# A hybrid block's input projection: column tiles in pairs by one level of Strassen's product

## The chip, the core and the metric

The kernel runs on one core of a Trainium2 chip. Five engines work side by side and wait for each other by semaphores: TensorE (PE, matmuls), VectorE (DVE), ScalarE (ACT), GpSimd (POOL), and SyncE (SP), which issues the transfers between memory (HBM) and the on-chip buffer (SBUF). PE writes its results into eight banks of PSUM. The metric is device microseconds (us) of the core.

## The reference

x has 1024 tokens of 1024 channels, in float32. What is computed:

```python
h = rmsnorm(x, norm_gain)                       # per token, over 1024 channels
q, f_logit, i_in, z_a, u, gate_b, gate_c, z_b = split(h @ w_in)   # 8 parts of 512 columns
f = lb + (1 - lb) * sigmoid(f_logit);  k = 1 - f
# group A, 4 heads of 128: S_t = diag(f_t) S_{t-1} + k_t v_t^T (v = i_in),  o_t = S_t^T q_t
o_a = grouped_rmsnorm(o_a, hgrn_norm_gain, 4) * silu(z_a)
# group B: causal convolution over 3 tokens, channel by channel
y_b = gate_b * conv3(gate_c * u)
o_b = grouped_rmsnorm(y_b, conv_norm_gain, 8) * silu(z_b)
x = x + concat(o_a, o_b) @ w_out
out = rmsnorm(x, final_norm_gain)
```

The input projection is 1024 x 1024 by 1024 x 4096: 32 column tiles of 128.

## The kernel before

Every product is made from rounded parts: an operand is split into a high part (a cast on ACT) and a low part (source minus high part, on DVE), and a product takes three matmuls: high by high, high by low, low by high. "Main matmul" is one of these, 512 columns wide.

*Stage v* (lines 116 to 173) computes i_in (called v) with tokens on the partitions, the contraction outermost, in all eight PSUM banks: 192 main matmuls, while x and the first weights arrive. x carries the norm's gain but is not normalised: the sums of squares of its rows come from eight further loads of x (`row_sum`, L152), and rst, the inverse root mean square of each token, is applied to the results, as a scale on ACT where tokens are on the partitions, or as a product with R (rst along the columns, L219) where channels are.

*Heads* (`head`, L239): for each of four heads the tiles f and q by `project` (L226: 24 main matmuls for one column tile and one half of the tokens, into one of four banks `psa`), then the recurrence's chain on DVE (sigmoid, a scan L257, four reciprocals L260) and POOL. The recurrence itself is eight small steps on PE.

*Convolution* (`conv`, L338): tiles u, c, b, z of four channel tiles. The norm of y (L362) sums squares over channels by two matmuls with a block of ones (`bones`), for which the squares are split as well (POOL, L377 and L381), then a root on ACT, a reciprocal of 128 x 512 on DVE (L368) and a product.

*Gate z_a and output projection* (L446 to L517): z_a with tokens on the partitions, transposes, then 16 output tiles of 24 main matmuls, residual and final norm; the last tile in two halves.

PE and SP work in the order of the program (`manual_schedule`); a scheduler sets the order on ACT, DVE and POOL. Each engine takes its instructions in its fixed order, so one that waits holds back what stands behind it. `Stream` (L37) sets PE's order: `pe.mm` is a main matmul, `pe.later(n, fn)` puts small steps behind n more of them (STEP 13 between steps of a recurrence, NLAG 44 from a conv tile to its norm's sums). Weights come by `fetch` in 512 KB units, six of them on chip.

Of the kernel before, what the change touches and what calls it, by code (L numbers as in the profile page):

```python
# [16 lines left out]
P = 128  # L17
# [4 lines left out]
W = 512  # L22
# [3 lines left out]
WB = 6       # weight units on chip  # L26
# [29 lines left out]

@with_exitstack
def hybrid_block(ctx: ExitStack, tc: tile.TileContext, xT, x, wtok, wcol, wout, cols, hgain, fgain, out):
# [25 lines left out]
    ga = const.tile([P, W], F32, name="ga")  # L84

# [1 line left out]
    units = [("v", kp, wtok[0, kp]) for kp in range(4)]  # L87
    for h in range(NH):
        units += [("f", h, wcol[2 * h + 1]), ("q", h, wcol[2 * h])]
    for j in range(4):  # L90
        units += [(c, j, wcol[8 + 4 * j + i]) for i, c in enumerate("ucbz")]
    units += [("za", kp, wtok[1, kp]) for kp in range(4)]
    units += [(f"o{n}", kp, wout[n, kp]) for n in range(2) for kp in (2, 3, 0, 1)]
    split, issued = {}, [0]

    def split_part(hi, lo, raw):
        A.copy(hi, raw)
        V.tensor_tensor(lo, raw, hi.bitcast(F32), op=ALU.subtract)  # L98

    def fetch(upto):  # L100
        while issued[0] < min(upto, len(units)):
            c, i, src = units[issued[0]]
            raw = stage.tile([P, 2 * W], F32, tag="st", name=f"raw_{c}{i}")
            hi = wpool.tile([P, 2 * W], F32R, tag="wh", name=f"wh_{c}{i}")
            lo = wpool.tile([P, 2 * W], F32R, tag="wl", name=f"wl_{c}{i}")
            nc.sync.dma_start(raw, src)
            split_part(hi, lo, raw)
            split[c, i] = hi, lo
            issued[0] += 1

    def need(c, i):
        pos = next(p_ for p_, u in enumerate(units) if u[0] == c and u[1] == i)
        fetch(pos + WB)
        return split[c, i]

# [1 line left out]
    pv = [(psa if t < 4 else psb).tile([P, W], F32, tag="ps", name=f"pv{t}") for t in range(NT)]  # L117

    def split_x(k, raw, t0, t1):
        g = col[:, C_NG + k:C_NG + k + 1]  # L120
        rv = raw.rearrange("p (t c) -> p t c", c=P)[:, t0:t1]
        A.activation(XH[:, t0:t1, k, :], rv, AF.Copy, scale=g)
        V.scalar_tensor_tensor(XL[:, t0:t1, k, :], rv, g, XH[:, t0:t1, k, :].bitcast(F32), op0=ALU.mult,
                               op1=ALU.subtract)

    rstart = const.tile([P, W], F32, name="rstart")
    V.memset(rstart[:, :P], 0.0)
    V.memset(rstart[:, P:], 0.0)
    for _ in range(NWARM):  # warms TensorE up while the first loads run
        T.matmul(pv[NT - 1][:, :P], rstart[:, :P], rstart[:, :P], start=True, stop=True)  # L130

    raw = stage.tile([P, S], F32, tag="st", name="rawx0")
    w0 = stage.tile([P, 2 * W], F32, tag="st", name="raw_v0")
    hi = wpool.tile([P, 2 * W], F32R, tag="wh", name="wh_v0")
    lo = wpool.tile([P, 2 * W], F32R, tag="wl", name="wl_v0")
    split["v", 0] = hi, lo
# [12 lines left out]
    ssx = const.tile([P, NT], F32, name="ssx")

    def row_sum(t):
        xr = stage.tile([P, D], F32, tag="st", name=f"xr{t}")  # L152
        nc.sync.dma_start(xr, x[t * P:(t + 1) * P, :])
        A.activation(xr, xr, AF.Square, accum_out=ssx[:, t:t + 1])

    for k in range(NK):
        if k:
            raw = stage.tile([P, S], F32, tag="st", name=f"rawx{k}")
            nc.sync.dma_start(raw, xT[k])
            if k % 2 == 0:  # L160
                fetch(k // 2 + 1)
            split_x(k, raw, 0, NT)
            row_sum(k - 1)
            if k == NK - 1:
                row_sum(k)
                fetch(5)
        hi, lo = split["v", k // 2]
        wh = hi[:, (k % 2) * W:(k % 2 + 1) * W]
        wl = lo[:, (k % 2) * W:(k % 2 + 1) * W]
        for t in range(NT):  # L170
            pe.mm(pv[t], XH[:, t, k, :], wh, start=(k == 0), stop=False)
            pe.mm(pv[t], XH[:, t, k, :], wl, start=False, stop=False)
            pe.mm(pv[t], XL[:, t, k, :], wh, start=False, stop=(k == NK - 1))

# [1 line left out]
    ident = const.tile([P, P], F32, name="ident")  # L176
    make_identity(nc, ident)
# [61 lines left out]
    def head(h):  # L239
# [58 lines left out]
        def combine(pr):  # L298
# [269 lines left out]
```

## Time and profile before

| | us |
|---|---|
| device time, median of 3 runs | 504.24 (502.28 to 506.0) |
| span of the profiled execution | 500.7 |
| own device time of the profiled execution | not among the times shown; the median is 3.54 above its span |
| PE busy | 491.8 (98%) |
| DVE busy | 257.6 (51%) |
| ACT busy | 172.7 (34%) |
| POOL busy | 157.4 (31%) |

The span runs from the first to the last instruction of one execution. Busy time is the time in which an engine executes; register and semaphore instructions don't count. An engine with a low share can still hold back another where its work is due at a certain moment.

### The profile page before, as it was taken

The page shows a single profiled execution, that of the slowest core. Times are in us where ns is not written, and L with a number is a line of the kernel's source. Part 1 is how long each engine was busy: PE and PEld are TensorE (multiplying, and loading weights), DVE is VectorE, ACT ScalarE, POOL GpSimd, SP SyncE. Part 2 cuts the span into 40 slices and gives each one's busy share as a digit, 9 for nine tenths or more (in the row PEclk, how much of TensorE's full clock was granted, in tenths as well). Part 3 has the DMA queues.
Part 4 walks back from the last instruction along what each step waited for, and adds up shares of the span by engine and source line. Part 5 has one row for each costly group of instructions (what it writes and reads, how often), then busy time and mean ns, then how long its engine had stood idle before and what let it go on. Part 6 is the DMA issues. An engine that isn't in the chain of part 4 may idle for free. (4 is left out here: it accounts for less than half of the span.)

```text
span 500.7 us, 5886 instructions
## 1 busy us (share of the span) xinstructions
PE 491.8 (98%) x2288; PEld 402.9 (80%) x2288; DVE 257.6 (51%) x363; ACT 172.7 (34%) x301; POOL 157.4 (31%) x143
## 2 busy tenths in 40 slices
PE   9999999999999999999999999999999999999995
PEld 7778887888888888888888888888888888888884
DVE  4342688948668335285647266552933461132323
ACT  5557722233223223170243127122722341123322
POOL 1000044524315003353658975233432122211000
PEclk9999999999999999999999999999999999999998
DMA  7778621110011110202111111112030171001342
GB/s 218 245 255 258 220 87 43 42 43 13 31 43 43 43 43 8 65 13 85 43 43 42 43 42 42 47 47 76 8 119 0 42 232 42 2 0 63 126 159 93
DMA packets 12699, 38.93 MB, mean 78 GB/s; under 512 B 1536, under 2 KB 2048, under 8 KB 12672
## 3 DMA queue, kind: packets, MB, share of 16 engines
q1 hardware_dynamic: 12672, 38.56, 23.2%
q8 instruction: 18, 0.29, 0.3%
q14 instruction: 9, 0.07, 0.0%
HBM read 34.36 MB, written 4.19 MB: 77 GB/s over the span
## 5 line engine op out<-in xcount | busy, mean ns | idle before, releaser
L44 PE MATMUL po<-wh_o,XL 128*128 128x512 f32 (+1 forms) x136 | 52.0, 382 | 0.0
L44 PE MATMUL po<-wl_o,XH 128*128 128x512 f32 (+1 forms) x136 | 52.0, 382 | 0.0
L44 PE MATMUL po<-wh_o,XH 128*128 128x512 f32 (+1 forms) x136 | 51.9, 382 | 0.0
L253 POOL TENSOR_SCALAR k<-f 128x512 f32<-128x512 f32 x8 | 5.0, 621 | 88.2 <-DVE f L251 88.2
L44 PEld LDWEIGHTS po<-wl_o,XH 128*128 128x128 f32 x136 | 25.5, 188 | 5.5
L44 PEld LDWEIGHTS po<-wh_o,XH 128*128 128x128 f32 x136 | 25.5, 188 | 5.4
L44 PEld LDWEIGHTS po<-wh_o,XL 128*128 128x128 f32 x136 | 25.5, 188 | 5.4
L368 DVE RECIPROCAL rs<-rs 128x512 f32<-128x512 f32 x8 | 26.8, 3353 | 3.7 <-ACT rs L367 3.5
L260 DVE RECIPROCAL ei<-e 128x128 f32<-128x128 f32 x32 | 27.1, 909 | 0.3
L44 PE MATMUL pp_f<-XH,wl_f 128*128 128x512 f32 x64 | 26.3, 411 | 0.0
L44 PE MATMUL pv<-wl_v,XH 128*128 128x512 f32 x64 | 25.6, 400 | 0.6 <-DVE wl_v L98 0.5
L44 PE MATMUL pp_q<-XH,wh_q 128*128 128x512 f32 x64 | 26.0, 407 | 0.0
L44 PE MATMUL pp_f<-XL,wh_f 128*128 128x512 f32 x64 | 26.0, 406 | 0.0
L44 PE MATMUL pp_q<-XH,wl_q 128*128 128x512 f32 x64 | 25.8, 403 | 0.0
L44 PE MATMUL pp_q<-XL,wh_q 128*128 128x512 f32 x64 | 25.8, 403 | 0.0
L44 PE MATMUL pp_f<-XH,wh_f 128*128 128x512 f32 x64 | 25.8, 403 | 0.0
L44 PE MATMUL pza<-wl_za,XH 128*128 128x512 f32 x64 | 25.7, 402 | 0.0
L354 POOL TENSOR_TENSOR cu<-us,R 128x512 f32<-128x512 f32 x8 | 11.3, 1418 | 45.9 <-DVE us L353 45.7
L44 PE MATMUL pv<-wh_v,XH 128*128 128x512 f32 x64 | 25.7, 401 | 0.0
L44 PE MATMUL pp_u<-XH,wl_u 128*128 128x512 f32 x64 | 25.6, 400 | 0.0
L44 PE MATMUL pp_c<-XH,wh_c 128*128 128x512 f32 x64 | 25.5, 399 | 0.0
L44 PE MATMUL pp_u<-XL,wh_u 128*128 128x512 f32 x64 | 25.5, 399 | 0.0
(181 smaller groups left out, 1261.1 us busy)
## 6 DMA issues: line engine op xcount, KB each, us to landing
xr<-x SPq DMA_DIRECT2D x8, 512.0 KB, 4.4
raw_o<-wout SPq DMA_DIRECT2D x8, 512.0 KB, 3.2
xo<-x SPq DMA_DIRECT2D x16, 256.0 KB, 3.4
rawx<-xT SPq DMA_DIRECT2D x7, 512.0 KB, 4.1
out<-y SPq DMA_DIRECT2D x7, 512.0 KB, 2.8
raw_f<-wcol SPq DMA_DIRECT2D x4, 512.0 KB, 3.7
raw_q<-wcol SPq DMA_DIRECT2D x4, 512.0 KB, 5.1
raw_u<-wcol SPq DMA_DIRECT2D x4, 512.0 KB, 3.2
```

What stands on the lines that cost most here:

```text
L44: self.T.matmul(*args, **kw)
L253: G.tensor_scalar(kk, f, -1.0, 1.0, op0=ALU.mult, op1=ALU.add)
L260: V.reciprocal(ei[:, c0:c0 + W // 4], e[:, c0:c0 + W // 4])
L354: G.tensor_tensor(cu[:, 2 + o0:2 + o0 + W], us[hf], rs, op=ALU.mult)
L368: V.reciprocal(rs2, rs2)
```

## The change

x is normalised on the chip before the projections, and 28 of the 32 column tiles (all but v's four) are computed in 14 pairs by Strassen's product in Winograd's form: x transposed is cut into four blocks A11, A12, A21, A22 (two halves of channels by two halves of tokens), a pair's weights into B11, B12, B21, B22 (two halves of channels by two column tiles).

- *x* comes in 16 tiles of 256 KB. In stage v it is used as before, without rst, but one half of the tokens after the other (4 banks each). Its squares (ACT) are added up on POOL; `stats` turns them into rst with four one-column matmuls for each half; `normalise` multiplies x in place by the gain and rst. The eight row loads, R, and its products are gone.
- *Blocks of x*: `split_a` and `x_sums` build seven blocks A11, A12, A22, S1 = A21 + A22, S2 = S1 − A11, S3 = A11 − A21, S4 = A12 − S2, each of four tiles, split into high and low parts (sums on DVE and POOL, casts on ACT, subtractions on DVE or POOL).
- *Weights of a pair* (`prep`): four loads of 256 KB, four sums on POOL (T1 = B12 − B11, T2 = B22 − T1, T3 = B22 − B12, T4 = B21 − T2), seven casts on ACT and seven subtractions on DVE. There are five buffers for high parts, five for low parts, four for raw tiles.
- *A pair* (`pair`): seven products of 12 main matmuls in three banks pb, pa, pd. Three sums are kept: m1 (A11·B11), u2 (pb after S2·T2), m5 (S1·T1) are copied by ACT to SBUF. Each of the four results is a bank plus such a copy, an addition on DVE (L328), or the bank alone. Bank pb takes S2·T2 after m1's copy, S3·T3 after u2's copy, and A22·T4 after the addition in `c22`.
- *Pairs in order*: for each head h the pairs (f, q), (u, c), (b, z) of head h and channel tile h; then z_a in two pairs. So a head and a channel tile now alternate, where all heads came first.
- *Small steps*: STEP 18, NLAG 32 for the first half of a tile and 44 for the second. The norm of a head runs on POOL in the pairs behind it. The output projection loads its weights in 256 KB tiles, and its first job (not the seventh) has two tiles.

```diff
-STEP = 13    # main matmuls between the steps of a head's recurrence
-NLAG = 44    # main matmuls between a conv tile and its norm's sums
...
+STEP = 18
+NLAG = 32, 44
...
-    stage = ctx.enter_context(tc.tile_pool(name="stage", bufs=3))
-    wpool = ctx.enter_context(tc.tile_pool(name="wpool", bufs=WB))
-    tmp = ctx.enter_context(tc.tile_pool(name="tmp", bufs=9))
+    hip = ctx.enter_context(tc.tile_pool(name="hip", bufs=5))
+    lop = ctx.enter_context(tc.tile_pool(name="lop", bufs=5))
+    rawp = ctx.enter_context(tc.tile_pool(name="rawp", bufs=4))
+    tpool = ctx.enter_context(tc.tile_pool(name="tpool", bufs=3))
+    tmp = ctx.enter_context(tc.tile_pool(name="tmp", bufs=11))
...
-    XH = const.tile([P, NT, NK, P], F32R, name="XH")
-    XL = const.tile([P, NT, NK, P], F32R, name="XL")
-    R = const.tile([P, S], F32, name="R")
...
+    XH = const.tile([P, 7, 4, W], F32R, name="XH")
+    XL = const.tile([P, 7, 4, W], F32R, name="XL")
...
+    def v_parts(hf, k):
+        b = ((S2, S1), (S3, S4))[hf][k // 4]
+        return XH[:, b, k % 4, :], XL[:, b, k % 4, :]
...
+    def split(hi, lo, src, eng=V):
+        A.copy(hi, src)
+        eng.tensor_tensor(lo, src, f32(hi), op=ALU.subtract)
...
-        xr = stage.tile([P, D], F32, tag="st", name=f"xr{t}")
-        nc.sync.dma_start(xr, x[t * P:(t + 1) * P, :])
-        A.activation(xr, xr, AF.Square, accum_out=ssx[:, t:t + 1])
...
+        A.activation(hi, at, AF.Copy, scale=g)
+        V.scalar_tensor_tensor(lo, at, g, f32(hi), op0=ALU.mult, op1=ALU.subtract)
+        sq = qk.tile([P, W], F32, tag="kh" if k == 0 else "qh", name=f"sx{hf}_{k}")
+        A.activation(sq, at, AF.Square)
+        if k == 0:
+            sqacc[hf] = sq
+        else:
+            G.tensor_tensor(sqacc[hf], sqacc[hf], sq, op=ALU.add)
...
+        ps = psb.tile([P, 4], F32, tag="ps", name=f"pst{hf}")
+        for t in range(4):
+            T.matmul(ps[:, t:t + 1], sqacc[hf][:, t * P:(t + 1) * P], ones, start=True, stop=True)
+        r = rst[:, 4 * hf:4 * hf + 4]
+        with tc.high_priority(AHEAD):
+            A.activation(r, ps, AF.Sqrt, bias=epsc, scale=1.0 / D)
+            V.reciprocal(r, r)
+    def normalise(hf):
+        pr = psb.tile([P, W], F32, tag="ps", name=f"pr{hf}")
+        for t in range(4):
+            T.transpose(pr[:, t * P:(t + 1) * P], rst[:, 4 * hf + t:4 * hf + t + 1].to_broadcast([P, P]), ident)
+        for k in range(NK):
+            at = x_at(hf, k)
+            with tc.high_priority(AHEAD):
+                V.scalar_tensor_tensor(at, at, col[:, C_NG + k:C_NG + k + 1], pr, op0=ALU.mult, op1=ALU.mult)
+    def split_a(b, eng):
...
+            if which == 0:
+                V.tensor_tensor(a22, a21, a22, op=ALU.add)
+                split(XH[:, S1, k, :], XL[:, S1, k, :], a22)
+                V.tensor_tensor(a21, a11, a21, op=ALU.subtract)
+                G.tensor_tensor(a11, a22, a11, op=ALU.subtract)
+                split(XH[:, S2, k, :], XL[:, S2, k, :], a11)
+            elif which == 1:
+                split(XH[:, S3, k, :], XL[:, S3, k, :], a21)
+            else:
+                G.tensor_tensor(a12, a12, a11, op=ALU.subtract)
+                split(XH[:, S4, k, :], XL[:, S4, k, :], a12)
...
+    pe.later(7 * 12 + 2, lambda: stats(0))
+    pe.later(7 * 12 + 10, lambda: normalise(0))
...
+        load_wv(k)
+        load_x(0, k)
+        v_mms(0, pa, k)
+    for k in range(NK):
+        load_x(1, k)
+    pe.later(20, lambda: stats(1))
+    pe.later(28, lambda: normalise(1))
...
+        for i, name in enumerate(("b11", "b12", "b22", "b21")):
+            b.append(rawp.tile([P, W], F32, tag="raw", name=f"{name}_{n}"))
+            nc.sync.dma_start(b[i], wpair[n, i])
...
+        def part(name, src):
+            hi = hip.tile([P, W], F32R, tag="hi", name=f"h{name}_{n}")
+            lo = lop.tile([P, W], F32R, tag="lo", name=f"l{name}_{n}")
+            split(hi, lo, src)
+            ops[name] = hi, lo
+        part("B11", b11)
+        G.tensor_tensor(t1, b12, b11, op=ALU.subtract)
+        G.tensor_tensor(t2, b22, t1, op=ALU.subtract)
+        part("B21", b21)
+        part("T2", t2)
+        part("T1", t1)
+        G.tensor_tensor(t3, b22, b12, op=ALU.subtract)
+        part("T3", t3)
+        G.tensor_tensor(t4, b21, t2, op=ALU.subtract)
+        part("T4", t4)
+        part("B22", b22)
+        wops[n] = ops
...
+    def product(ps, a, w, first):
...
+        b = bank("pb")
+        product(b, A11, ops["B11"], True)
+        m1 = keep("m1", b)
+        a = bank("pa")
+        product(a, A12, ops["B21"], True)
+        c11(a, m1)
+        product(b, S2, ops["T2"], False)
+        u2 = keep("u2", b)
+        if n + 1 < npair:
+            prep(n + 1)
+        elif mid is not None:
+            mid()
+        d = bank("pd")
+        product(d, S1, ops["T1"], True)
+        m5 = keep("m5", d)
+        product(b, S3, ops["T3"], False)
+        c22(b, m5)
+        product(d, S4, ops["B22"], False)
+        c12(d, u2)
+        product(b, A22, ops["T4"], False)
+        c21(b, None)
...
+        pair(n, forget(0), query(1), forget(1), query(0))
         for hf in range(2):
...
-            V.tensor_tensor(fl, pf, rs, op=ALU.mult)
...
-            pc = project("c", j, hf)
-            V.tensor_tensor(us[hf], pc, us[hf], op=ALU.mult)
-            G.tensor_tensor(cu[:, 2 + o0:2 + o0 + W], us[hf], rs, op=ALU.mult)
...
+        pair(n, lambda ps, t: add(us[0], ps, t), on_c1, on_u1, on_c0)
...
+        def on_b(hf):
+            def on(ps, t):
+                nm = f"{j}_{hf}"
+                y = conv_y(j, hf)
+                b = t512(f"b{nm}")
+                if t is None:
+                    V.tensor_tensor(y, ps, y, op=ALU.mult)
+                else:
+                    add(b, ps, t)
+                    V.tensor_tensor(y, y, b, op=ALU.mult)
+                G.tensor_tensor(b, y, y, op=ALU.mult)
+                sh = tmp.tile([P, W], F32R, tag="sqh", name=f"sh{nm}", bufs=1)
+                A.copy(sh, b)
+                sl = tmp.tile([P, W], F32R, tag="sql", name=f"sl{nm}", bufs=1)
+                G.tensor_tensor(sl, b, f32(sh), op=ALU.subtract)
+                pe.later(NLAG[hf], lambda: norm(hf, sh, sl))
...
+                add(z, ps, t)
...
+        pair(n, on_b(0), on_z(1), on_b1, on_z(0))
...
+    for k in range(NK):
+        v_mms(1, tiles, k)
+        if k == 0:
+            prep(0)
+        if k == 2:
+            split_a(A11, G)
+            split_a(A12, G)
+        if k == 3:
+            split_a(A22, V)
+            x_sums(0)
+            x_sums(1)
+    v_out(1, tiles)
+    x_sums(2)
...
+    for h in range(NH):
+        head(h, 3 * h)
+        conv_in(h, 3 * h + 1)
+        conv_out(h, 3 * h + 2)
...
-    r0 = vo
+    groups = [[0, 1]] + [[t] for t in range(2, NT)]
```

The order on three engines, as built (names: hB11 is the high part of a pair's B11, lT2 a low part, and so on; mb holds raw x at first, later the conv tiles; a number behind a name is the pair's, or a buffer's).

ACT at the end of stage v, around the root that makes rst. Before:

```order
L122 ACTIVATE XH_81<-rawx7_360,col_87 128x8x128
L154 ACTIVATE xr6_364,ssx_131<-xr6_364 128x1024
L154 ACTIVATE xr7_367,ssx_131<-xr7_367 128x1024
L195 ACT_TABLE_LOAD
L195 ACTIVATE rst_84<-ssx_131,epsc_420 128x8
L97 CAST wh_f0_371<-raw_f0_370 128x1024
L216 ACTIVATE vo_85<-pv0_89,rst_84 128x512
```

After:

```order
L119 CAST hB11_0_435<-b11_0_423 128x512
L147 ACTIVATE sx1_3_348<-mb_91 128x512
L147 ACTIVATE sx1_4_354<-mb_91 128x512
L162 ACT_TABLE_LOAD
L162 ACTIVATE rst_89<-pst0_298,epsc_93 128x4
L205 ACTIVATE vo_90<-pv0_97,rst_89 128x512
```

The root stood behind the last row sums of all tokens and a stage's worth of PE work; for the first half of the tokens it now stands behind a cast of pair 0's weights and squares of the second half, and PE needs it before the stage's second half.

DVE around the norm's reciprocal, channel tile 0. Before:

```order
L390 TENSOR_TENSOR z0_0_1833<-pp_z0_0_1801,R_83 128x512
L368 RECIPROCAL rs20_0_1825<-rs20_0_1825 128x512
L369 SCALAR_TENSOR_TENSOR y0_0_1662<-y0_0_1662,col_87,rs20_0_1825 128x512
L368 RECIPROCAL rs20_1_1863<-rs20_1_1863 128x512
L390 TENSOR_TENSOR z0_1_1871<-pp_z0_1_1839,R_83 128x512
```

After, in pair 2 and in pair 3:

```order
L491 RECIPROCAL rs20_0_1212<-rs20_0_1212 128x512
L328 TENSOR_TENSOR z0_1_1220<-pb_2_1049,m5_2_1192 128x512
L120 TENSOR_TENSOR lT2_3_1152<-t2_3_1139,hT2_3_1151 128x512
...
L353 MEMSET f1_0_1308 128x8
L355 SCALAR_TENSOR_TENSOR e1_0_1316<-f1_0_1308,rstart_95 128x512
L358 RECIPROCAL ei1_0_1318<-e1_0_1316 128x128 x4
L362 COPY gt1_1277<-e1_0_1316 128x8
L491 RECIPROCAL rs20_1_1397<-rs20_1_1397 128x512
L328 TENSOR_TENSOR qh1_1_1279<-pb_3_1280,m5_3_1405 128x512
```

Behind the reciprocal there stood a reading of a bank that has three others beside it; now the addition that frees pb stands there, and in pair 3 the scan and reciprocals of the next head stand ahead of both.

POOL from the end of a channel tile to the norm's low part sl. Before:

```order
L377 TENSOR_TENSOR sq0_1_1789<-y0_1_1716 128x512
L381 TENSOR_TENSOR sl0_1_1793<-sq0_1_1789,sh0_1_1791 128x512
```

After:

```order
L504 TENSOR_TENSOR b0_1_1269<-mb_91 128x512
L270 TENSOR_TENSOR t1_4_1349<-b12_4_1343,b11_4_1341 128x512
L445 TENSOR_TENSOR vo_90<-vo_90,ssa_405 128x4x128 x2
L523 TENSOR_TENSOR mb_91<-mb_91,z0_0_1251 128x512
L531 TENSOR_TENSOR mb_91<-mb_91,z0_1_1220 128x512
L508 TENSOR_TENSOR sl0_1_1274<-b0_1_1269,sh0_1_1272 128x512
L271 TENSOR_TENSOR t2_4_1351<-b22_4_1345,t1_4_1349 128x512
L275 TENSOR_TENSOR t3_4_1350<-b22_4_1345,b12_4_1343 128x512
L351 TENSOR_SCALAR kh1_0_1312<-f1_0_1308 128x512
```

Between the square and sl there stood nothing; now five steps stand there, and behind them the next pair's sums and the k that the next head's scan waits for.

ACT around the copy of u2, in pair 3 (after):

```order
L119 CAST hB21_4_1359<-b21_4_1347 128x512
L302 COPY u2_3_1339<-pb_3_1280 128x512
```

Neither stood there before; the cast's buffer is the one that T1 of pair 3 leaves.

## Rows read from the trace of the kernel before

**Rows 1.** The page, part 1: busy time, share, instructions of each engine.

```profile
PE 491.8 (98%) x2288; PEld 402.9 (80%) x2288; DVE 257.6 (51%) x363; ACT 172.7 (34%) x301; POOL 157.4 (31%) x143
```

**Rows 2.** PE's waits: waiting tile and line, releaser; us, count, longest.

```profile
PE pv L130 <- DVE rstart L127: 1.1, 1, 1.1
```

**Rows 3.** Windows: stretch, length; PE, PEld, DVE, ACT, POOL busy; granted clock, DMA, GB/s.

```profile
0.00:51.20 51.20, 49.50 (x208) 39.80 (x209) 18.89 (x32) 30.91 (x44) 1.56 (x12) 1.00 0.77 245
51.20:165.80 114.60, 113.53 (x594) 95.50 (x594) 84.37 (x150) 35.62 (x88) 40.51 (x40) 1.00 0.18 59
...
403.90:494.60 90.70, 90.68 (x417) 73.98 (x415) 27.43 (x49) 25.55 (x55) 12.82 (x10) 1.00 0.26 88
```

**Rows 4.** A window of the output projection, PE's matmuls into po alone.

```profile
430.00:480.00 50.00, 50.00 (x216) 1.00 0.18 63
```

**Rows 5.** Timeline: start, length, engine, line; the first and last main matmul.

```profile
4.91 0.79 PE L44 MATMUL pv<-wh_v,XH 128*128 128x512 f32 x1
...
494.31 0.28 PE L44 MATMUL po<-wh_o,XL 128*128 128x256 f32 x1
```

**Rows 6.** A window of stage v while tiles arrive, columns as in rows 3.

```profile
24.00:36.00 12.00, 11.97 (x52) 9.37 (x51) 5.08 (x4) 7.18 (x9) 0.00 (x0) 1.00 0.76 252
```

**Rows 7.** Groups by line and shape: count, busy us, mean ns, idle time before.

```profile
L356 ACT ACTIVATE y<-cu,col 128x512 f32<-128x512 f32 x8 | 5.8, 725 | 23.9 <-POOL cu L354 23.9
L490 ACT ACTIVATE xo<-vo 128x512 f32<-128x512 f32 x8 | 5.1, 634 | 29.3 <-DVE vo L489 29.3
L98 DVE TENSOR_TENSOR wl_v<-raw_v,wh_v 128x512 fp32r<-128x512 f32 x2 | 1.4, 693 | 0.8 <-ACT wh_v L97 0.8
L381 POOL TENSOR_TENSOR sl<-sq,sh 128x512 fp32r<-128x512 f32 x8 | 10.4, 1299 | 12.7 <-ACT sh L379 12.7
L347 DVE TENSOR_TENSOR us<-pp_u,R 128x512 f32<-128x512 f32 x8 | 5.5, 686 | 11.5 <-PE pp_u L44 11.5
L367 ACT ACT_TABLE_LOAD x7 | 9.0, 1283 | 0.1
L195 ACT ACTIVATE rst<-ssx,epsc 128x8 f32<-128x8 f32 x1 | 0.3, 300 | 0.0
L196 DVE RECIPROCAL rst<-rst 128x8 f32<-128x8 f32 x1 | 0.2, 203 | 3.7 <-ACT rst L195 3.7
L97 ACT CAST wh_v<-raw_v 128x512 fp32r<-128x512 f32 x2 | 1.2, 619 | 2.5 <-DMA raw_v<-wtok 2.5
L368 DVE RECIPROCAL rs<-rs 128x512 f32<-128x512 f32 x8 | 26.8, 3353 | 3.7 <-ACT rs L367 3.5
L367 ACT ACTIVATE rs<-pss,epsc 128x512 f32<-128x512 f32 x8 | 5.5, 688 | 1.1 <-PE pss L365 1.0
L253 POOL TENSOR_SCALAR k<-f 128x512 f32<-128x512 f32 x8 | 5.0, 621 | 88.2 <-DVE f L251 88.2
L257 DVE TENSOR_TENSOR_SCAN e<-f,rstart 128x512 f32<-128x512 f32 x8 | 9.8, 1225 | 0.3
L260 DVE RECIPROCAL ei<-e 128x128 f32<-128x128 f32 x32 | 27.1, 909 | 0.3
```

**Rows 8.** Timeline of DVE in the convolution, columns as in rows 5.

```profile
242.83 2.29 DVE L98 TENSOR_TENSOR wl_z<-raw_z,wh_z 128x1024 fp32r<-128x1024 f32 x1 [0.16 <-ACT wh_z L97]
245.05 1.52 DVE L357 SCALAR_TENSOR_TENSOR y<-cu,col,y 128x512 f32<-128x512 f32 x1
```

**Rows 9.** Timeline of POOL in the same stretch.

```profile
242.75 1.29 POOL L354 TENSOR_TENSOR cu<-us,R 128x512 f32<-128x512 f32 x1
244.00 2.02 POOL L401 TENSOR_TENSOR sqa<-vo 128x512 f32<-128x512 f32 x1
```

**Rows 10.** Windows behind the last matmul, columns as in rows 3.

```profile
497.00:498.00 1.00, 0.00 (x0) 0.00 (x0) 0.00 (x0) 0.00 (x0) 0.00 (x0) 0.67 0.44 172
498.00:499.00 1.00, 0.00 (x0) 0.00 (x0) 0.00 (x0) 0.00 (x0) 0.00 (x0) 0.50 0.92 352
```

More of the change, by code (lines that the diff above doesn't have):

```diff
@@ L96, in split_part @@
[L96 to L109, printed above, removed]
@@ L126, in hybrid_block @@
[L126 to L136, printed above, removed]
@@ L176, in hybrid_block @@
-    ident = const.tile([P, P], F32, name="ident")
-    make_identity(nc, ident)
+    epsc = const.tile([P, 1], F32, name="epsc")
+    ones = const.tile([P, 1], F32, name="ones")
+    rstart = const.tile([P, W], F32, name="rstart")
+    ident = const.tile([P, P], F32, name="ident")
+    pa = [psa.tile([P, W], F32, tag="ps", name=f"pv{t}") for t in range(4)]
+    V.memset(rstart, 0.0)
+    V.memset(epsc, EPS)
+    V.memset(ones, 1.0)
+    for _ in range(NWARM):
+        T.matmul(pa[3][:, :P], rstart[:, :P], rstart[:, :P], start=True, stop=True)
@@ new lines, in v_mms, with v_out @@
+    def v_mms(hf, tiles, k):
+        xh, xl = v_parts(hf, k)
+        wh, wl = wvs[k]
+        for t, p_ in enumerate(tiles):
+            c = slice(t * P, (t + 1) * P)
+            pe.mm(p_, xh[:, c], wh, start=(k == 0), stop=False)
+            pe.mm(p_, xh[:, c], wl, start=False, stop=False)
+            pe.mm(p_, xl[:, c], wh, start=False, stop=(k == NK - 1))
+    def v_out(hf, tiles):
+        for t, p_ in enumerate(tiles):
+            A.activation(vo[:, 4 * hf + t, :], p_, AF.Copy, scale=rst[:, 4 * hf + t:4 * hf + t + 1])
@@ new lines, in product, with pair, bank, keep @@
+    def product(ps, a, w, first):
+        wh_, wl_ = w
+        more = {} if first else {"skip_group_check": True}
+        for k in range(4):
+            c = slice(k * P, (k + 1) * P)
+            pe.mm(ps, wh_[:, c], XH[:, a, k, :], start=(first and k == 0), stop=False, **more)
+            pe.mm(ps, wh_[:, c], XL[:, a, k, :], start=False, stop=False, **more)
+            pe.mm(ps, wl_[:, c], XH[:, a, k, :], start=False, stop=(k == 3), **more)
+    def pair(n, c11, c22, c21, c12, mid=None):
+        ops = wops.pop(n)
+        def bank(name):
+            return psa.tile([P, W], F32, tag="ps", name=f"{name}_{n}")
+        def keep(name, ps):
+            t = t512(f"{name}_{n}")
+            A.copy(t, ps)
+            return t
+        b = bank("pb")
[19 more added lines that the diff above has]
+        c21(b, None)
@@ new lines, in a_split @@
+    def a_split(todo):
+        for j, hf, z in todo:
+            hi = mixed(XH, j, hf)
+            A.copy(hi, z)
+            V.tensor_tensor(mixed(XL, j, hf), z, f32(hi), op=ALU.subtract)
+    p7 = psa.tile([P, W], F32, tag="ps", name="pv7")
+    v_out(0, pa)
+    tiles = pb + [p7]
+    for k in range(NK):
[9 more added lines that the diff above has]
+            x_sums(1)
@@ new lines, in hybrid_block, with load_out @@
+    v_out(1, tiles)
+    x_sums(2)
+    wo = {}
+    OUT_ORDER = [4, 5, 6, 7, 0, 1, 2, 3]
+    def load_out(n, k):
+        i = OUT_ORDER.index(k)
+        if n == 1:
+            hi, lo = [part[:, (S3, A22)[i // 4], i % 4, :] for part in (XH, XL)]
+        elif i >= 5:
+            hi, lo = [part[:, S4, i - 5, :] for part in (XH, XL)]
+        else:
+            hi = hip.tile([P, W], F32R, tag="hi", name=f"woh{k}")
+            lo = lop.tile([P, W], F32R, tag="lo", name=f"wol{k}")
+        raw = rawp.tile([P, W], F32, tag="raw", name=f"wo{n}_{k}")
+        nc.sync.dma_start(raw, wout[n, k])
+        split(hi, lo, raw)
+        wo[n, k] = hi, lo
@@ L477, in hybrid_block @@
     residual(1)
+    gf = [tpool.tile([P, W], F32, tag="t", name=f"gf{n}") for n in range(2)]
+    for n in range(2):
+        nc.sync.dma_start(gf[n], fgain[n * W:(n + 1) * W].partition_broadcast(P))
     for i, (n, g) in enumerate(jobs):
```

502 lines of the change are left out of this document (250 added, 252 removed).

## The prediction, made before the changed kernel ran

> **What bounds the kernel now.** I read the busy shares first [rows 1]: TensorE (PE) works 491.8 of the 500.7 us of the span, the vector engine (DVE) about half of it, ScalarE (ACT) and GpSimd (POOL) a third each. The waits of PE [rows 2] say the same from the other side: the first group of its list is the 1.1 us ahead of the warm-up. By stage (v, the heads, the output projection [rows 3]) PE is busy nearly all the time and the granted clock is 1.00, the higher level (2.4 GHz). So only PE's work counts now, and every other engine has room; what one main matmul costs comes from a stretch that holds nothing but output-projection matmuls [rows 4]: 216 records, two of them cut by the edges, 50/214 = 0.2336 us. I carry the span of the one profiled execution, 500.7, and what lies around it, 504.24 − 500.7 = 3.5 us to the median of the three times shown; the profiled execution has no other time.
>
> **The change, part by part.**
>
> *Saved.* Each of 14 pairs took 4 x 24 = 96 matmuls and takes 7 x 12 = 84. 168 x 0.2336 = **39.2 us**, all on PE, which sets the end.
>
> *Start, +2.3.* The first main matmul stands at 4.9 us [rows 5]. It now needs a whole tile of x cast and scaled, with its square between on ACT (0.73 and 0.63 [rows 7]): +1.3. Eight one-column matmuls for the row sums: not in the trace, bounded by nothing and by a main matmul each, 8 x 0.2336 = 1.9; a column is far less than 512, but each loads its weights, so +1.
>
> The rest are waits, since PE now depends on engines which had room. Two prices come first. A whole-tile subtraction takes DVE 0.69 and POOL 1.30 [rows 7]. When both have inputs in SBUF they take turns: DVE's subtraction at 242.83 lasts 2.29 and ends 1.08 after POOL's ends; POOL's next, issued at 244.00, lasts 2.02 and ends at 246.02, 0.90 after DVE's; DVE's next, issued at 245.05, ends 0.55 after that [rows 8, 9]. So I price a couple at 0.60 + 1.15 = **1.75 us** (bounds: 1.30, side by side, and 2.0). DVE operations with a PSUM input keep 0.69.
>
> *First statistics, 5.4.* x's first half is normalised on chip; PE's transposes of rst at matmul 94 stand at 6.2 + 94 x 0.2336 + 1 = 29.1 us. In the order of ACT the square root stands behind squares of the second half; the one of tile 4 needs a buffer that POOL's addition frees, and this addition stands behind t1 of the first pair, whose input is the 26th tile of 262 KB on SP's queue: 6.8 MB at 252 GB/s [rows 6] are 27.0, with 1.5 (an estimate) for the start and the landing 28.5. Then two POOL steps in turn with DVE 3.5, square 0.6, table load 1.28, root and reciprocal of the four columns 0.5: 34.4. Bounds 0 (the root comes first in time) and 6. The removed row sums were eight loads of 512 KB on this queue; they lay under stage v and give nothing.
>
> *Second statistics, 4.4.* PE reaches them 24 matmuls later, about 40.1; POOL has nine subtractions and additions left from 32.0 on, 9 x 1.30 = 11.7 and a turn of 0.8: 44.5. Bounds 2 and 5.
>
> *First pair, 10.* Normalisation ends near 53 on DVE: 44.5, a root and a reciprocal 0.5, its table 1.28, four transposes 1, eight passes of 0.69. Then all operands of pair 0 and the seven blocks of x are built: by the order 29 SBUF subtractions on DVE and 11 on POOL, 29 x 0.60 + 11 x 1.15 = 30.1, to 83. PE, whose stage v ended at 51.2 before [rows 3] and now at 63.3 with the terms above, wants the last part of S2 in its third product, at 63.3 + 33 x 0.2336 = 71.0. That is 12; I take 10 for what may be built in another order. Bounds 0 and 13.
>
> *Copies of u2, 5.0.* The fifth product writes over bank pb, so u2's copy must be done. In pairs 0, 3, 6 and 9 it stands on ACT behind the cast of the next B21, whose buffer is free only after the fourth product: cast and copy, 2 x 0.62 = 1.24, four times. Elsewhere the copy stands ahead, under 2.8 us of the fourth product: nothing (1.24 more each if it didn't).
>
> *Reciprocal in the conv-out pairs, 7.2.* c22's addition reads pb, and PE's last product waits for it: it has 12 matmuls, 2.8 us. On DVE it stands behind the norm's reciprocal, 3.35. Table 1.28 + root 0.69 + 3.35 + addition 0.69 = 6.0 from the sums on; PE has 16 matmuls and two small ones, 4.2. 1.8 each, four pairs. Bounds: 0 (the root comes earlier) and 3.4.
>
> *Sums of the second norm, 7.6.* They are placed 44 matmuls (10.3 us) behind the pair and need POOL's sl, seventh in a row of POOL steps: 0.69 + 7 x 1.30 + four turns of DVE 2.4 = 12.2. 1.9, four times; 0 without turns, 3.5 at the top.
>
> *Head pairs 3, 6, 9, 11.7.* From the end of the pair before: POOL 12.2, two more subtractions 2.6, k 0.62, DVE's scan 1.23, four short reciprocals 3.64, the norm's reciprocal 3.35, addition 0.69, less 0.07 for each of some six hand-overs [rows 8]: 23.9. PE is there after 72 matmuls, 16.8, and its waits of 1.9 and 1.24: 20.0. 3.9 each; bounds 0 and 6.
>
> *Costed at nothing.* The sums that replace the products with R read PSUM as these did (0.69). SP: 256 KB tiles in place of 512 KB, 131 issues for 88; its share after stage v is under 0.3 [rows 3], so transfers lie hidden; without that cover a tile is 1.0 us. The head's steps: 18 matmuls apart for 13, more room. The second gate pair's split lies under 36 matmuls (8.4 us) of the first output job; four casts and subtractions are some 5 us, which is the price without the cover.
>
> Sum of waits: 5.4 + 4.4 + 10 + 5.0 + 7.2 + 7.6 + 11.7 = **51.3**. Span 500.7 − 39.2 + 2.3 + 51.3 = 515.1; time **518.6**.
>
> **A rule against the change.** In this trace the granted clock left 1.00 once, behind the last matmul (which ended at 494.6 [rows 5]): 0.67 in the slice from 497 and 0.50 from 498, the lower level (1.2 GHz) [rows 10]. PE had been busy until then and did nothing from then on. Six of the waits above (5.4, 4.4, 10 and the three of 3.9) would be the first long pauses within the work. What a matmul costs after such a pause is not in this trace: nothing at the least; at the most a whole product of twelve at half speed each time, 6 x 2.8 = 16.8; the middle is 8.4. I leave it out of the sum and keep it as a rival.
> The Trainium skill, "TensorE: Matmul & The Clock Gate", section "HAM oscillation — how this bites in real kernels", says that waits between bursts of matmuls put the engine back to its lower clock, and that the next burst starts slow each time. By that rule the sum would be the rival's, below; the trace of before agrees in its one pause, at the end, and shows no burst behind one.
>
> **The rivals.**
> *PE stays fed (not slower).* One mechanism with one point: if the addition that frees pb ends within the 2.8 us of the sixth product in every pair, and the buffers of the operands come as early, the waits fall away: 500.7 − 39.2 + 2.3 + 3.5 = 467.3; with half of the waits, 493. For it: no engine but PE is busy over 51% [rows 1]. Against: 3.35 us reciprocals stand ahead of that addition in seven pairs, and they alone are longer than 2.8. It decides itself in the conv-out pairs.
> *No turns.* If DVE's and POOL's subtractions run side by side, the terms become 4.4 (two steps of 1.30), 3.6, 2 (29 x 0.69 = 20, to 73), 5.0, 7.2, 0 (POOL's row 9.8) and 3 x 3.5 = 10.5 (that row 2.4 shorter, PE 1.9 earlier): 32.7, time 500.0, with 492 to 508 about it. For it: DVE's 0.69 on this shape in stage v, where POOL hardly works [rows 3], is the length they could keep. Against: [rows 8, 9].
> *The clock falls*: 518.6 + 8.4 = 527, up to 536. Against: other engines' work between keeps the pauses short if my waits are too large.
> That the 168 matmuls aren't saved can't be: they are counted in the program's order on PE.
>
> **How the numbers follow.** A measurement here tells about 1%, 5.0 us, from no change. Chances: forecast 0.47 (509.5 to 526), all slower; clock 0.09, slower; no turns 0.25, of which 0.09 is faster, 0.14 the same, 0.02 slower; fed 0.16, faster; 0.03 for others, the same (all estimates, by how the rows speak above). Faster 0.25, same 0.17, slower 0.58. The predicted time is the forecast's, 518.6. The range holds the forecast, the no-turn case and the lower part of the clock's: 0.47 + 0.25 + 0.06, and the top of the fed case: 492 to 532.
>
> **What would show it.** Right: main matmuls still 0.23 apart and 168 fewer; PE waits named by the statistics in stage v (about 5 and 4 us), by lower halves in pair 0, by c22's addition behind a 3.35 us reciprocal, by u2's copy behind a cast, by sl before the norm's sums; DVE and POOL subtractions longer than 0.69 and 1.30. Wrong: PE's waits under 20 us in sum, or at other places (a late tile, a recurrence step); the clock's digits under 9 would show the rival.

## The result and the profile after

The changed kernel takes **528.5 us** (median of 4 runs, 527.0 to 530.3) against 505.0 for the kernel before in the same comparison: ratio 1.047, 95% interval 1.041 to 1.053. It is slower, as forecast (518.6, range 492 to 532), by 10 us more than forecast. The profiled execution took 528.66, of which the span is 526.9.

The page, part 1 and the clock's row of part 2; it answers to [rows 1].

```profile
span 526.9 us, 6115 instructions
PE 475.2 (90%) x2136; PEld 384.0 (73%) x2136; DVE 363.0 (69%) x523; ACT 249.6 (47%) x469; POOL 246.5 (47%) x191
PEclk9978985999998899998899998899999999999999
```

PE has less to do, and is idle or slow elsewhere: its share fell from 98% to 90%, and the granted clock, which was at 1.00 through the work before [rows 3], dips in the start and in each of the three places where a head begins behind a channel tile. PE's waits (waiting tile and line, releaser; us, count, longest), where before hardly any were [rows 2]. In this list sl is the low part of the conv norm's squares, qh and z are the additions of `c22` in a head's pair and in a conv-out pair, m and u are the copies m1 and u2, XL is a low part of a block of x, and sx and rst are the sums of squares and the inverse roots of the rows.

```profile
PE pss L487 <- POOL sl L508: 7.3, 4, 2.0
PE pr L168 <- DVE rst L163: 7.1, 1, 7.1
PE pb L48 <- DVE qh L328: 7.1, 3, 2.5
PE pb L48 <- DVE z L328: 6.3, 4, 1.6
PE pb L48 <- DVE XL L120: 5.2, 2, 3.5
PE pb L48 <- ACT m L302: 4.5, 1, 4.5
PE pb L48 <- ACT u L302: 4.0, 4, 1.0
PE pst L159 <- POOL sx L151: 1.2, 1, 1.2
```

With 1.1 in two smaller groups these are 43.8 us in 24 waits, all behind the warm-up; the kernel before had three there, of 0.7, 0.5 and 0.4, 1.6 in all. By stretch, columns as in [rows 3]:

```profile
72.00:96.00 24.00, 13.37 (x35) 8.89 (x36) 23.64 (x23) 11.33 (x19) 15.08 (x10) 0.64 0.16 44
96.00:165.80 69.80, 65.85 (x315) 53.65 (x313) 50.38 (x76) 32.25 (x64) 38.68 (x31) 1.00 0.15 42
165.80:403.90 238.10, 217.50 (x987) 176.10 (x988) 173.28 (x248) 113.17 (x212) 121.27 (x98) 0.96 0.14 40
403.90:494.60 90.70, 90.70 (x408) 73.94 (x407) 47.03 (x72) 39.02 (x74) 22.15 (x14) 1.00 0.29 99
```

The first row lies in the first pair: 35 matmuls in 24 us. In the last PE is fed and at the full clock, as before: the loss is in certain places. PE's last main matmul starts at 520.65, where it started at 494.31 [rows 5]: all of the difference lies ahead of it. One of the places, the beginning of the second head, on DVE and then on PE (start, length, engine, line):

```profile
168.88 3.39 DVE L358 RECIPROCAL ei<-e 128x128 f32<-128x128 f32 x4
172.18 0.11 DVE L362 COPY gt<-e 128x8 f32<-128x8 f32 x1
172.20 3.34 DVE L491 RECIPROCAL rs<-rs 128x512 f32<-128x512 f32 x1
175.46 0.63 DVE L328 TENSOR_TENSOR qh<-pb,m 128x512 f32<-128x512 f32 x1
```

```profile
176.14 0.51 PE L48 MATMUL pb<-XH,hT 128*128 128x512 f32 x1 [2.28 <-DVE qh L328]
...
177.47 0.63 PE L48 MATMUL pb<-XL,hT 128*128 128x512 f32 x1
177.90 0.63 PE L48 MATMUL pb<-XH,lT 128*128 128x512 f32 x1
```

c22's addition (qh) frees the bank that the last product wants; it stands behind the head's four short reciprocals and the norm's long one. Behind the wait the matmuls are 0.43 apart, where 0.2336 was normal [rows 4]: the granted clock is 0.50 (1.2 GHz) from 177 to 180 us.

**Where the 26.2 us of span went.** Saved −39.2; first main matmul at 5.30 for 4.91, +0.4; matmuls of the row sums, +1.8; waits +43.8, less the 1.6 that PE waited before; slow matmuls +16.9 (what each loses against 0.2336, summed over nine stretches at the lower clock: 1.3, 1.4 and 4.6 in the start, and two of about 1.6 in each of pairs 3, 6 and 9). That makes 22.1; the other 4.1 isn't broken down. The two dozen restarts would make most of it (an estimate): the matmul ahead of a wait counts as busy for 0.39, where the next one would have started 0.23 behind it, and the first spacing behind a wait is about 0.1 longer.

### The profile page after: what moved, and what is told of

It reads as the page before. It is cut to its first block, busy times and chain, and to the rows that moved or that the text cites. A ratio compares the mean times of both kernels' runs of the same rounds, so it can differ in the third digit from the quotient of the medians.

```text
span 526.9 us, 6115 instructions
## 1 busy us (share of the span) xinstructions
PE 475.2 (90%) x2136; PEld 384.0 (73%) x2136; DVE 363.0 (69%) x523; ACT 249.6 (47%) x469; POOL 246.5 (47%) x191
## 5 line engine op out<-in xcount | busy, mean ns | idle before, releaser
L48 PE MATMUL pb<-XH,hT 128*128 128x512 f32 x168 | 73.5, 438 | 21.9 <-DVE qh L328 7.1
L48 PE MATMUL pb<-XL,hT 128*128 128x512 f32 x168 | 72.5, 432 | 5.4 <-DVE XL L120 5.2
L48 PE MATMUL pb<-XH,lT 128*128 128x512 f32 x168 | 70.5, 420 | 0.0
L119 ACT CAST hT<-t 128x512 fp32r<-128x512 f32 x56 | 34.5, 617 | 58.8 <-PE pb L48 42.3
L120 DVE TENSOR_TENSOR lT<-t,hT 128x512 fp32r<-128x512 f32 x56 | 44.5, 800 | 10.2 <-ACT hT L119 10.2
L120 DVE TENSOR_TENSOR lB<-b,hB 128x512 fp32r<-128x512 f32 x42 | 35.0, 841 | 21.9 <-ACT hB L119 21.9
L277 POOL TENSOR_TENSOR t<-b,t 128x512 f32<-128x512 f32 x14 | 23.4, 1668 | 48.7 <-DVE lT L120 48.0
L48 PE MATMUL po<-XH 128*128 128x512 f32 (+1 forms) x96 | 35.7, 372 | 0.0
L48 PE MATMUL po<-XL,XH 128*128 128x512 f32 (+1 forms) x96 | 35.7, 372 | 0.0
L48 PE MATMUL po<-XH,XL 128*128 128x512 f32 (+1 forms) x96 | 35.7, 372 | 0.0
L271 POOL TENSOR_TENSOR t<-b,t 128x512 f32<-128x512 f32 x14 | 20.4, 1456 | 6.2 <-DVE lT L120 6.2
```

What stands on the lines that cost most here:

```text
L48: self.T.matmul(*args, **kw)
L119: A.copy(hi, src)
L120: eng.tensor_tensor(lo, src, f32(hi), op=ALU.subtract)
L271: G.tensor_tensor(t2, b22, t1, op=ALU.subtract)
L277: G.tensor_tensor(t4, b21, t2, op=ALU.subtract)
```

## The experiments

Each is the changed kernel with the edit shown, unless said otherwise; in brackets stands the ratio to the kernel before, with its interval. The kernel before had medians from 503.2 to 505.0 in the four comparisons from which the times come, so a difference of under some 2 us between two of these runs says little.

**1. The order of pairs.**

```diff
-        head(h, 3 * h)
-        conv_in(h, 3 * h + 1)
+        conv_in(h, 3 * h)
+        head(h, 3 * h + 1)
```

(and the weights' pairs in the same order).

> The changed kernel with one thing altered: the order of the pairs within a head's three, (u, c) first, then (f, q), then (b, z). Theory A (the waits of pairs 3, 6 and 9 arise where the end of a channel tile's norm, POOL's squares and the 3.35 us reciprocal, meets the next head's chain of k on POOL, scan and four reciprocals on DVE): with (u, c) between them the waits on sl, u2 and qh, 2.0 + 1.0 + 2.3 three times, fall under 1 us each, and with them the stretches at the lower clock behind them; 504 to 516 us. Rival B (DVE at 69% and POOL at 47% are too full in any order): waits of the same sum at other places, 525 to 531 us.

Measured 511.65 (ratio 1.014, 1.010 to 1.019). Its main waits behind the start, and a window from the end of pair 3 to the beginning of pair 9:

```profile
PE po L406 <- DVE st L413: 6.7, 4, 1.7
PE pb L48 <- ACT u L302: 3.8, 3, 1.3
PE pb L48 <- DVE qh L328: 2.8, 3, 0.9
PE pb L48 <- DVE z L328: 2.7, 4, 0.7
```

```profile
166.00:300.00 134.00, 124.94 (x589) 100.58 (x588) 117.50 (x158) 61.06 (x123) 75.47 (x59) 1.00 0.15 42
```

Theory A: 17 us from order alone, with DVE busier (75% of the span for 69%), not less busy. The waits on sl are gone, qh is 0.9, the clock stays at 1.00. Two details missed: u2's copy still costs 1.3, and a new wait of 1.7 on the recurrence's state came up.

**2 and 3. One chain at a time.** The reciprocal away (2), and the second rounding of the squares away (3):

```diff
-            A.activation(rs2, pss, AF.Sqrt, bias=epsc, scale=1.0)
-            V.reciprocal(rs2, rs2)
+            A.activation(rs2, pss, AF.Abs_reciprocal_sqrt, bias=epsc, scale=1.0)
```

```diff
-                G.tensor_tensor(b, y, y, op=ALU.mult)
-                A.copy(sh, b)
-                G.tensor_tensor(sl, b, f32(sh), op=ALU.subtract)
+                A.activation(sh, y, AF.Square)
...
-            T.matmul(pss, bones, sl, start=False, stop=True)
```

(with two buffers for the squares instead of one).

> The norm's root (ACT) and reciprocal (DVE, 3.35 us) are one ACT operation, the inverse root; eight reciprocals fewer. Theory A (two chains in a row, each of which can hold PE: the reciprocal before c22's addition, and POOL's row up to sl): the z waits, 1.6 four times, go, PE comes earlier to the sums of the second norm, and waits there longer, 3.5 to 5 for 2.0; net 6 to 11 less, 517 to 523 us. Rival C (the reciprocal is behind the z, qh and sl waits alike): 18 to 25 less, 503 to 511 us.

> The norm's squares are made by ACT, rounded once, and their low parts are left out: 16 operations of POOL (y squared and sl), and 8 small matmuls (1.9 us of PE) fewer; the reciprocal stays. Theory A (two chains in a row): the waits on sl, 7.3 in sum, go, PE comes earlier to c22's bank in pairs 3, 6, 9 and waits there longer, 3.5 to 5 for 2.3; net 5 to 11 less, 517 to 524 us. Rival D (POOL's row is behind all of these waits): 18 to 25 less, 503 to 511 us.

Measured 525.2 (1.041, 1.037 to 1.045) and 521.9 (1.033, 1.027 to 1.038). First the largest wait of the one, then the two of the other:

```profile
PE pss L487 <- POOL sl L507: 17.7, 4, 4.6
```

```profile
PE pb L48 <- DVE qh L328: 11.6, 3, 4.4
PE pb L48 <- DVE z L328: 7.2, 4, 1.8
```

Theory A both times: without the reciprocal the waits on z and qh are gone and those on sl are 4.6 for 2.0; without the second rounding those on sl are gone and qh is 4.4 for 2.3. Experiment 2 stayed 2 us above its range, and its gain of 3.3 is little more than the scatter; around its longer wait the clock averages 0.59 from 160 to 170.

**4. Idle matmuls ahead of the waits of pairs 3, 6 and 9.**

```diff
+    def fill(ps, count):
+        for _ in range(count):
+            T.matmul(ps, XH[:, A11, 0, :P], XH[:, A11, 0, :], start=True, stop=True)
...
+        if n in (3, 6, 9):
+            fill(a, 10)
```

(and in the same way four ahead of the fifth product and eight ahead of the norm's sums).

> In pairs 3, 6 and 9 matmuls whose results nobody reads are put ahead of the three waits: 8 before the norm's sums, 4 before the fifth product, 10 before the last; 66 in all, 15.4 us of PE work, nothing else altered. Theory E (the granted clock falls because PE pauses there): it stays at 1.00 in the six stretches of these pairs, matmuls behind them are 0.23 apart, and the time is 522 to 530 us, since the added work lies in the pauses. Rival F (the clock falls for another reason, such as how much the kernel does around these places): the six stretches stay at 0.50, and what of the added work does not fit into the pauses comes on top, 532 to 544 us.

Measured 526.1 (1.043, 1.039 to 1.048), with 66 more matmuls. The same five microseconds of the changed kernel and of this one (columns as in [rows 3]):

```profile
176.00:181.00 5.00, 4.86 (x14) 3.86 (x15) 3.14 (x6) 0.38 (x1) 2.30 (x2) 0.66 0.00 0
```

```profile
176.00:181.00 5.00, 5.00 (x22) 4.00 (x22) 3.90 (x6) 2.28 (x3) 2.67 (x2) 1.00 0.01 3
```

Theory E: 22 matmuls for 14, and the clock at 1.00. It is the pause that lowers the clock here. The gain is 2.4 us, within the scatter of the two (525.3 to 527.9 against 527.0 to 530.3). And PE's slack ahead of that product is now the ten matmuls, 2.34, and a wait of 1.57: 3.9 us, what the forecast had for it. In the changed kernel it showed as 2.3, because PE, slowed since the wait before, came 1.6 later.

The execution profiled is the slowest of this run's four, and pair 4 of it has a longer wait on the recurrence's state (st) than the changed kernel has anywhere:

```profile
PE po L414 <- DVE st L421: 3.4, 3, 2.5
```

Beside it the clock is at 0.50 from 193.9 to 197.3. From the z wait of one conv-out pair to the next it takes 81.0 us over this place, where the changed kernel takes 78.8, and 77.5 over each of the two others, pairs 6 and 9: there 1.3 us come back of the 3.1 that the slow matmuls had cost.

**5. Both short chains together** (edits 2 and 3).

> The two edits together: the norm's inverse root as one ACT operation, and its squares made by ACT and rounded once. Alone they gave 525.2 and 521.9 us, where the changed kernel takes 528.5. Theory A (two chains end one behind the other, and taking one away only moves PE's wait to the other: the waits on sl became 4.6 each without the reciprocal, those on qh 4.4 each without the second rounding): together they give much more than their sum, 504 to 511 us, with under 1 us left of each sl, z and qh wait. Rival (the engines are too full, and each edit gives what work it takes away): the sum of the two, 528.5 - 3.3 - 6.6 = 518.6, 516 to 521 us.

Measured 503.3 (0.999, 0.996 to 1.002): 25.2 us less than the changed kernel, where the two alone gave 3.3 and 6.6.

```profile
PE pb L48 <- DVE qh L328: 6.0, 3, 2.0
```

Theory A in size (0.7 under its range); the qh wait, which was to fall under 1, is 2.0, since the chain of k with its four reciprocals still stands ahead of it.

**6. The sums of weight blocks left out.**

```diff
-        G.tensor_tensor(t1, b12, b11, op=ALU.subtract)
-        G.tensor_tensor(t2, b22, t1, op=ALU.subtract)
```

(and so for t3 and t4: four subtractions in each of 14 pairs, 56 in all, and not the 32 of the expectation). The products take unsummed blocks in their place, so this kernel's input projection is another one.

> The four sums of weight blocks of a pair are left out (32 POOL subtractions of 1.6 us; the products take unsummed blocks in their place, so the input projection is another one); the splits, the products, the norm and the order of pairs stay. Theory A with POOL's side of it (in pairs 3, 6 and 9 the sums stand between the norm's squares and the next head's k, and make DVE's copies wait in turns): the waits on sl and qh fall to under 1 us each and the time is 506 to 514 us. Rival H (the reciprocal of 3.35 us and the chain of k alone hold PE, the sums lie in the gaps): 521 to 526 us.

Measured 507.4 (1.007, 1.004 to 1.009), 21 us less. sl waits 0.8 in sum, but qh went up:

```profile
PE pb L48 <- DVE qh L324: 8.6, 3, 2.9
PE pb L48 <- DVE z L324: 6.3, 4, 1.6
PE pss L483 <- POOL sl L504: 0.8, 3, 0.3
```

The time is theory A's, its picture only half: POOL's added work is what held sl, and the reciprocal, in pairs 3, 6 and 9 with the chain of k, goes on holding z and qh, as rival H said of those two. Not all of the 21 us is sl's: the waits on u2 fell as well (1.0 for 4.0), and so did some of the start's.

**7. The start: root and reciprocal of the row norm as one step of ACT.**

```diff
-            A.activation(r, ps, AF.Sqrt, bias=epsc, scale=1.0 / D)
-            V.reciprocal(r, r)
+            A.activation(r, ps, AF.Abs_reciprocal_sqrt, bias=epsc, scale=1.0 / D)
```

> One operation of the changed kernel's start: the two halves' inverse roots are made by ACT in one step, where ACT made a root and DVE a reciprocal (two DVE operations of 0.16 us fewer). Theory A (the first statistics' wait of 7.1 us is the reciprocal's place in DVE's queue, behind eight low parts of 11.5 us in sum, not the late tile of x): the wait falls to under 1.5 us and the stretch at the lower clock behind it goes; part of it comes back at the first pair, whose parts wait for the eight multiplications and the sums on DVE: 520 to 525 us. Rival (the first pair's operands are what the start waits for in the end): the wait moves whole to the first pair, 526 to 530 us.

Measured 528.1 (1.049, 1.044 to 1.053): nothing gained. DVE of the changed kernel first, then of this run, then this run's PE:

```profile
24.60 11.53 DVE L145 SCALAR_TENSOR_TENSOR XL<-mb,col,XH 128x512 fp32r<-128x512 f32 x8
...
36.66 0.16 DVE L163 RECIPROCAL rst<-rst 128x4 f32<-128x4 f32 x1
```

```profile
25.85 11.62 DVE L145 SCALAR_TENSOR_TENSOR XL<-mb,col,XH 128x512 fp32r<-128x512 f32 x8
...
39.07 5.34 DVE L171 SCALAR_TENSOR_TENSOR x<-x,col,pr 128x512 f32<-128x512 f32 x8
```

```profile
32.43 0.65 PE L167 MATMUL pr<-ident,rst 128*128 128x128 f32 x4 [1.00 <-ACT rst L162]
44.56 1.84 PE L159 MATMUL pst<-ones,sx 128*128 128x1 f32 x8 [6.46 <-DVE x L171]
76.53 0.50 PE L48 MATMUL pb<-XH,hT 128*128 128x512 f32 x1 [4.74 <-ACT m L301]
```

As theory A said, a reciprocal of 0.16 us had stood behind eight low parts of 11.5; without it PE waits 1.0 for 7.1. But the eight multiplications stand behind the same low parts: the second statistics wait 6.5 for 1.2, and the first pair begins where it did (76.5 for 76.3). The rival has the time. The second half's eight multiplications begin at 50.42 for 50.14 in the changed kernel: the chain that leads to them, over DVE, PE and ACT, takes as long as it did.

**8. Versions put together.** Both have the swapped order, the inverse root, and another start: the mean squares of each half are eight accumulating matmuls, and there the orders of ACT, DVE and POOL are written out. The second also has the single rounding of experiment 3. The core of the start:

```diff
+        T.matmul(pms[hf], oneb, sqs[hf, k], start=(k == 0), stop=(k == NK - 1))
+            A.activation(pms[hf], pms[hf], AF.Abs_reciprocal_sqrt, bias=epsc, scale=1.0)
...
+    with tc.manual_schedule(engines={mybir.EngineType.Activation, mybir.EngineType.DVE, mybir.EngineType.Pool}):
```

> A version put together: pairs in the order (u, c), (f, q), (b, z); the norm's inverse root as one ACT operation; at the start, the mean squares by matmuls that add up over the eight tiles with a block of 1/1024, the inverse root on ACT, and ACT, DVE and POOL in a written order, in which the squares of the second half and the first pair's parts stand ahead of what nobody waits for. From the run with the swapped order (511.7 us): waits of 0.8 + 6.2 + 0.8 + 4.7 + 1.7 + 4.2 = 18.4 us stand in its first 90 us, and 0.7 + 0.9 of z and qh in every three pairs. If these waits are only of order (theory A), a third to two thirds of the 18.4 goes, and half of the lower clock behind them: 492 to 501 us, faster than the kernel before by 1 to 2%. Rival B (DVE and POOL are full over the first 90 us, so that order gives little): 504 to 510 us.

> The same version, and the norm's squares made by ACT and rounded once (16 POOL operations and 8 matmuls of 0.23 us fewer). Theory A: with the pairs swapped no wait on sl is left to lose, so that only the matmuls (1.9 us) and some turns of POOL and DVE go: 2 to 6 us less than the version without it, 488 to 497 us. Rival B: as much as alone, 6.6 us less, or more.

Measured **491.7** (0.976, 0.970 to 0.982) and **488.0** (0.967, 0.962 to 0.972), 0.3 under the first's range and at the lower end of the second's; only the second's interval lies wholly below 0.98. The page and the main waits of the faster one:

```profile
PE 459.6 (95%) x2136; PEld 374.7 (77%) x2136; DVE 332.3 (69%) x518; ACT 246.6 (51%) x472; POOL 198.4 (41%) x157
PEclk9999989999999999999999999999999999999998
```

```profile
PE po L416 <- DVE st L423: 6.4, 4, 1.6
PE pb L48 <- ACT u L310: 4.0, 5, 1.3
PE pb L48 <- DVE qh L338: 3.1, 4, 1.0
```

DVE's share is 69%, as in the changed kernel, while PE's is 95% for 90%; DVE's work is less too, 332 us for 363.

**9. What of this is the start's, and what the norm's alone.** The swapped order with both norm edits and the old start; and the kernel before with the norm edits.

> The swapped order of pairs, the inverse root as one ACT operation and the squares rounded once, with the start left as the changed kernel has it. Theory A (order and short chains take away the same waits, those of pairs 3, 6 and 9, each from its side): little more than either, 497 to 502 us (511.7 with the swap, 503.3 with the two short chains), and the written order of the start accounts for the other 9 to 14 us of the fastest version's 488.0. Rival (the two add up): 511.7 + 503.3 - 528.5 = 486.5, 485 to 491 us, and the start's order is worth next to nothing.

> The kernel before with the same two edits of the norm (one ACT operation for root and reciprocal, squares made by ACT and rounded once; 8 small matmuls fewer). If what these edits are worth lies in the waits that the change opened (theory A), the kernel before, where PE waits 1.6 us in sum, gains only the matmuls and a little: 500 to 503 us. Rival (the edits are worth as much there): 480 to 490 us.

Measured 503.0 (0.999, 0.997 to 1.001) and 500.35 (0.994, 0.991 to 0.997). The swap and the short chains remove the same waits (a microsecond above theory A's range), so the other start, its order and mean squares together, is worth the other 15.0 us of the 488.0. The kernel before gains 2.9 by the norm edits, near its eight matmuls of 0.2336, 1.9: it had few waits to lose (1.6). Against it the fastest version stands at 0.967/0.994 = 0.973.

## Why the forecast was right in sign and 10 us short

*Saved, 39.2, and start, 2.3.* Right: main matmuls at the full clock are still 0.23 apart; the start came to 0.4 + 1.8.

*Waits, 51.3 forecast, 43.8 measured.* First statistics 5.4, measured 7.1; second 4.4, 1.2; first pair 10, 9.7; u2 copies 5.0, 4.0; z 7.2, 6.3; sl 7.6, 7.3; qh 11.7, 7.1. The places held, and so did the turn of 1.75 (DVE's low parts in the first pair take 1.75 each, last section), so the rival without turns fell. By experiments: z is the reciprocal (2), sl POOL's row (3 and 6), qh both, and behind both the chain of k (5). One cause was wrong: the first statistics waited not for ACT's root behind a late tile (it started at 29.53) but for DVE's queue (7).

*The step that failed* is the one that left the clock out of the sum. The pauses were foreseen, the rule behind them named, and its price bounded at 16.8; then it was kept as a rival with a chance of 0.09, for want of a slow burst in the trace of before. Five of the six pauses came (the second statistics' was 1.2), and the clock fell there: 16.9 us of slow matmuls. That this lies beside the bound is luck, since the bound was six stretches of 2.8 and there were nine, eight of 1.3 to 1.7 and one of 4.6; three of them follow the waits on sl and u2 (2.0 and 1.0), which the rule was not applied to. The forecast of span, 515.1, plus 16.9, plus the 4.1 not broken down, less the 7.5 by which the waits and the 1.7 by which start and old waits fell short of it, is 526.9. So the time, 528.5, is the clock rival's (527, up to 536), and by the prediction's own sign (digits under 9) it is that rival which showed; the range holds it because its lower part was taken in. The Trainium skill, "TensorE: Matmul & The Clock Gate", section "HAM oscillation — how this bites in real kernels", says that the burst behind a wait starts at the lower clock. The trace agrees in part: behind the wait of 2.28 the first matmuls are 0.34, 0.24 and 0.33 apart and the next ones 0.43, and behind the four waits of 1.58 on z none is slow.

But 16.9 and 43.8 don't simply add up to what could be had back. In pairs 3, 6 and 9 the slow matmuls of the first stretch take 1.6 out of the wait that follows, and experiment 4, which kept the clock up there, got back 1.3 of 3.1 in each of the two pairs where no new pause came up. There the chains on DVE and POOL set most of the pace; PE's clock largely decides whether the time shows as waiting or as slow work.

*What the sum could not say.* It priced waits one by one, and most prices were near; as savings they are not terms. Two chains held PE in turn, so that taking out either gave 3.3 or 6.6 and both 25.2; taking 6 us off the start's first wait gave nothing. And a change of order, with no work removed, gave 17.

The rival in which PE stays fed (467.3) fell, and no run reached it. Of the 61 us between it and the changed kernel, order alone took away 17, and order, the shorter norm and the other start together 40; in that fastest version PE is at 95%.

## What to carry to other kernels

When a change takes work off the bound engine and gives it to others, ask not whether they have room in sum (DVE is at 69% in the changed kernel, and at 75% in experiment 1, which is 17 us faster) but what stands in their queues ahead of the one instruction that the bound engine waits for. Look for two chains that end one behind the other before you cut one, and expect little of cutting one alone. If the forecast has new pauses on TensorE, put slower matmuls behind them into the sum, as a range, and not beside it.

## What was not expected of the hardware

POOL and DVE don't always take turns. In the changed kernel one POOL subtraction lasts 7.63, where it takes 1.30 alone, while DVE's subtractions beside it run back to back at their full pace; then, after a gap in DVE's work, both take turns (POOL first, then DVE):

```profile
60.46 7.63 POOL L186 TENSOR_TENSOR x<-mb,x 128x512 f32<-128x512 f32 x1 [7.76 <-DVE mb L185]
68.16 1.30 POOL L191 TENSOR_TENSOR x<-x,x 128x512 f32<-128x512 f32 x1
69.42 3.42 POOL L186 TENSOR_TENSOR x<-mb,x 128x512 f32<-128x512 f32 x2
```

```profile
62.03 1.29 DVE L185 TENSOR_TENSOR mb<-x,mb 128x512 f32<-128x512 f32 x2
63.24 1.28 DVE L120 TENSOR_TENSOR XL<-mb,XH 128x512 fp32r<-128x512 f32 x2
...
68.77 1.24 DVE L120 TENSOR_TENSOR XL<-x,XH 128x512 fp32r<-128x512 f32 x1 [1.84 <-ACT XH L119]
71.64 1.75 DVE L120 TENSOR_TENSOR XL<-mb,XH 128x512 fp32r<-128x512 f32 x1
```

The same step lasts 7.62 and 7.63 in experiments 1 and 7. The Trainium skill, "SBUF — State Buffer", section "Who interferes with whom", says that a VectorE instruction with two SBUF inputs contends with a GpSimd instruction that reads SBUF, and that the order of issue decides which one blocks. The trace agrees that they contend; here POOL stood still over ten DVE instructions and more, until DVE paused. Why turns begin in one place and not in the other was not tested.

Short waits sufficed to bring the clock down in some places, and waits of the same length did not in others. Of the four waits of 1.80 on z in experiment 3 the first two are followed by matmuls 0.23 apart, the last two by 3.4 us at 0.50; here are the second and the third:

```profile
226.59 0.50 PE L48 MATMUL pb<-XH,hT 128*128 128x512 f32 x1 [1.80 <-DVE z L328]
...
227.63 0.39 PE L48 MATMUL pb<-XL,hT 128*128 128x512 f32 x1
```

```profile
304.15 0.50 PE L48 MATMUL pb<-XH,hT 128*128 128x512 f32 x1 [1.80 <-DVE z L328]
...
305.31 0.63 PE L48 MATMUL pb<-XL,hT 128*128 128x512 f32 x1
```

Of the three of 1.99 on qh in experiment 5 the first alone is followed by such a stretch, and in the fastest version one follows a wait of 1.42 that has one of 0.65 two microseconds ahead of it. So the length of one wait does not tell whether the clock falls; what else decides was not tested.
